# Hybrid attention layer: the two end blocks of each window share one transpose, GpSimd parts them again, and mixer B's projections stand in one planned line

## The chip, the core and the metric

The kernel runs on one core of one Trainium2 chip, in one launch. The metric is device time in microseconds (us); smaller is better. Times are medians of a few runs; the profile is one further execution, with every instruction's start and duration. Engines are PE (TensorE), DVE (VectorE), ACT (ScalarE), POOL (GpSimd) and SP (SyncE, which issues most of the transfers).

## The reference, cut to what matters

One decoder layer over 1024 tokens of width 1024. After the norm, one projection feeds two attention mixers. Mixer A (8 heads, 2 key/value groups) has three branches per query: compressed tokens (`cmp`), selected blocks (`slc`) and a sliding window of 512 keys (`win`). Mixer B (8 heads, 2 groups) has a sliding window of 128 keys (`swa`) with one learned sink per head that enters the softmax's sum alone. ALiBi distances are subtracted everywhere.

```python
def banded_attention(q, k, v, slopes, window, sinks=None):
    # 128-query blocks; keys t-window+1..t
    s = jnp.einsum('bgrnqd,bgnkd->bgrnqk', qb, kb) * (dh ** -0.5)
    valid = (dist >= 0) & (dist < window) & (kpos[:, None, :] >= 0)
    s = s - slopes[None, :, :, None, None, None] * dist.astype(jnp.float32)
    s = jnp.where(valid, s, NEG)
    if sinks is not None:
        p = jax.nn.softmax(jnp.concatenate([s, sink], axis=-1), axis=-1)[..., :-1]
    else:
        p = jax.nn.softmax(s, axis=-1)
    return jnp.einsum('bgrnqk,bgnkd->bgrnqd', p, vb)
...
o_win = banded_attention(qa, k_win, v_win, slopes_a, NSA_WINDOW)              # window 512
o_b = banded_attention(qb, kb_, vb_, slopes_b, SWA_WINDOW, sinks=sinks[l])    # window 128
```

For a 128-query block i, the window of 128 keys touches key blocks i-1 and i, and the window of 512 touches i-4 to i. In the oldest block only keys strictly above the diagonal (column j > row p) are inside the window; in block i only those with j <= p. So the two end blocks of a window together have exactly one valid key for each pair (p, j).

## The kernel before, in words

Every product of full precision is made of two parts in a rounded type: a high part and a low part (`hh`, `hl` of the input; `wh`, `wl` of the weights; `ph`, `pl` of the probabilities; V holds both halves side by side). Projections (lines L187 to L195, and L917 to L922 in `quarter`) are half blocks of 24 matmuls with 512 columns: 8 chunks of the depth, three products each.

Attention runs in four units: mixer B groups 0 and 1, then mixer A groups 0 and 1. A unit goes over its tasks (query block i, branch). A task has two steps:

- `scores`: for each of the group's four heads r, two matmuls (q with `kh` and `kl`) into a PSUM bank `s`; DVE adds the ALiBi distances and takes the row's minimum in one custom instruction (L797); ACT takes the exponential with the row's sum (L809); DVE takes the reciprocal (L813); POOL scales the row by it and by the branch's gate (L821). Distances and masks are in tables: `DC` (causal), `DW` (window of 512) and `DB` (window of 128); masked places hold 1e30.
- `weigh`: for each key block, four PE transposes (one per head, L858) into one bank `pt`; ACT copies that to `ph` (L864), DVE subtracts to get `pl` (L865); two PV matmuls of 512 columns (L866 with `ph`, L869 with `pl`) add to `pv`. After a query block's last branch, `finish` adds the two halves of `pv`, multiplies by the gate path (POOL, L880) and stores.

The `weigh` of a task is issued after the `scores` of the next. For `swa` the sink enters as the starting value of the minimum, and its term of the sum is made apart: subtract, exponential, add, then one reciprocal (L815 to L818). The rows of `slc`, and of every second `swa`, are in buffers `ps` (4 of 1024 columns), those of `win` and the other `swa` in `pw` (4 of 640 columns).

The order of each engine's queue is set when the kernel is built: attention has high priority, and projections of later stages fill PE between its steps. What limits them is `hold`: a projection may not stand before the attention matmul that lies `AHEAD` us back by a count of attention's columns (`mark`, `done`, `held`). In mixer A they stand in one line, `pieces`, cut into quarters of a half block (`Planned.quarter`), each with a due place; `pump` issues those that are due, and `owed` makes an attention step wait for a quarter that is `LAG` overdue. In mixer B, projections are issued whole after a task (`spread`, and a loop over the `late` ones).

`split_half` makes `wh` (a copy, ACT) and `wl` (a subtraction, POOL, L164) from each loaded half of weights.

## Time and profile before

| | |
|---|---|
| runs | 899.46, 900.00, 901.08 us; median 900.0 |
| profiled execution | 900.77 us, of which the span of instructions is 899.0 us |
| mean granted PE clock | 0.992 |
| mixer B's attention, first to last POOL scaling | 171.0 to 292.5 us |
| mixer A's attention | 292.5 to 694.6 us |
| POOL: weight halves `wl` (L164) | 102, 133.7 us in all |
| POOL: row scalings (L821), `ps` and `pw` and `pc` | 192 |

A row of the groups reads: line, engine, operation, output<-inputs, shapes, count, then busy us in all, mean ns of one, then idle us of the engine just before them and what ended it. A row of the timeline reads: start us, duration us, engine, line, operation, tiles, count, and in brackets the idle time before it with its releaser. Matmul durations overlap: the next one starts before the last has ended.

### The profile page before, as it was taken

To read this page: it belongs to the slowest core of one execution; us is meant where nothing else is said; L and a number is where in the kernel's file an instruction comes from. 1 tells how busy PE (TensorE), PEld (TensorE's weight loads), DVE (VectorE), ACT (ScalarE), POOL (GpSimd) and SP (SyncE) were. 2 spreads that over 40 slices of the span, in tenths; PEclk is the share of its full clock that TensorE was granted. 3 is DMA by queue.
4 is the path that set the end of the run, shared out by engine and by line. 5 is a ranking of instruction groups with operands and counts; after the bars stand their busy time and mean duration, and the time that the engine had idled before them with its cause. 6 is when DMAs were issued, how large, how long until landed. Compare 5 with 4: busy or idle time off the path is not lost.

```text
span 899.0 us, 14304 instructions
## 1 busy us (share of the span) xinstructions
PE 888.9 (99%) x4538; PEld 753.0 (84%) x4538; DVE 538.2 (60%) x1511; ACT 505.6 (56%) x1150; POOL 356.9 (40%) x428
## 2 busy tenths in 40 slices
PE   8999999999999999999999999999999999999997
PEld 7989888888888888888888888888887888887885
DVE  5866863465578677575585677566463372677322
ACT  6477732466676877565666777565464555442111
POOL 1000421365576866452544576453351366200000
PEclk7999999999999999999999999999999999999999
DMA  9873442342234332111222131211212677335432
GB/s 353 281 249 101 141 163 78 118 136 97 82 101 116 115 87 73 48 54 53 71 63 80 60 89 59 80 51 36 83 39 68 207 250 230 115 112 188 138 104 80
DMA packets 67087, 104.51 MB, mean 116 GB/s; under 512 B 8002, under 2 KB 25794, under 8 KB 67011
## 3 DMA queue, kind: packets, MB, share of 16 engines
q1 hardware_dynamic: 65856, 102.36, 35.1%
q10 hardware_dynamic: 1154, 1.23, 0.5%
q8 instruction: 36, 0.59, 0.3%
q14 instruction: 41, 0.33, 0.1%
HBM read 79.97 MB, written 19.92 MB: 111 GB/s over the span
## 4 chain that ended last, share of the span: by engine, by line
PE 95%; DVE 1%; DMA 1%; ACT 1%; issue 0%; POOL 0%; SPq 0%; DVEq 0%; POOLq 0%; ACTq 0%
PE b_pt L858 8%; PE b_pj L917 7%; PE b_pj L921 7%; PE b_pj L922 7%; PE b_pj L194 5%; PE b_pj L195 5%; PE b_pj L187 5%; PE b_s L790 5%; PE b_s L787 4%; PE b_pv L869 4%; PE b_pv L866 4%; PE b_s L1158 1%; PE b_s L1157 1%; PE b_s L1156 1%; PE b_s L1078 1%; PE b_s L1080 1%
## 5 line engine op out<-in xcount | busy, mean ns | idle before, releaser
L164 POOL TENSOR_TENSOR wl<-wraw,wh 128x512 fp32r<-128x512 f32 x102 | 133.7, 1313 | 137.7 <-ACT wh L161 86.6
L865 DVE TENSOR_TENSOR pl<-b_pt,ph 128x512 fp32r<-128x512 f32 x162 | 110.4, 687 | 63.2 <-ACT ph L864 62.3
L864 ACT CAST ph<-b_pt 128x512 fp32r<-128x512 f32 x162 | 93.8, 583 | 64.7 <-PE b_pt L858 51.2
L917 PE MATMUL b_pj<-hh,wh 128*128 128x512 f32 x288 | 117.6, 412 | 0.0
L922 PE MATMUL b_pj<-hh,wl 128*128 128x512 f32 x288 | 114.0, 396 | 0.0
L921 PE MATMUL b_pj<-hl,wh 128*128 128x512 f32 x288 | 113.1, 394 | 0.0
L821 POOL TENSOR_SCALAR ps<-ps,rr,gates 128x128 f32<-128x128 f32 (+7 forms) x64 | 52.7, 827 | 92.4 <-DVE rr L813 51.4
L194 PE MATMUL b_pj<-hl,wh 128*128 128x512 f32 x224 | 88.2, 394 | 0.0
L187 PE MATMUL b_pj<-hh,wh 128*128 128x512 f32 x224 | 88.0, 393 | 0.0
L195 PE MATMUL b_pj<-hh,wl 128*128 128x512 f32 x224 | 87.9, 393 | 0.0
L787 PE MATMUL b_s<-kh,q 128*128 128x256 f32 (+6 forms) x272 | 85.8, 323 | 0.0
L790 PE MATMUL b_s<-kl,q 128*128 128x256 f32 (+6 forms) x272 | 83.9, 316 | 0.0
L809 ACT ACTIVATE ps<-ps,mins 128x256 f32<-128x256 f32 (+7 forms) x96 | 64.9, 677 | 32.2 <-DVE mins L797 30.4
L161 ACT CAST wh<-wraw 128x512 fp32r<-128x512 f32 x94 | 57.5, 615 | 32.8 <-PE b_pj L194 11.7
L809 ACT ACTIVATE pw<-pw,mins 128x256 f32<-128x256 f32 (+4 forms) x96 | 60.7, 633 | 26.6 <-DVE mins L797 26.2
L869 PE MATMUL b_pv<-pl,V 128*128 128x512 f32 x162 | 67.5, 417 | 0.2
L866 PE MATMUL b_pv<-ph,V 128*128 128x512 f32 x162 | 65.3, 403 | 0.0
L922 PEld LDWEIGHTS b_pj<-hh,wl 128*128 128x128 f32 x288 | 54.1, 188 | 10.8
L921 PEld LDWEIGHTS b_pj<-hl,wh 128*128 128x128 f32 x288 | 54.4, 189 | 8.5
L880 POOL TENSOR_TENSOR ot<-ot,zt 64x512 f32<-64x512 f32 x32 | 41.2, 1288 | 49.9 <-DVE ot L879 41.0
L821 POOL TENSOR_SCALAR pw<-pw,rr,gates 128x640 f32<-128x640 f32 (+4 forms) x64 | 47.6, 748 | 32.4 <-DVE rr L813 18.0
L917 PEld LDWEIGHTS b_pj<-hh,wh 128*128 128x128 f32 x288 | 53.9, 189 | 7.5
(309 smaller groups left out, 2137.7 us busy)
## 6 DMA issues: line engine op xcount, KB each, us to landing
wraw<-in_w_blk SPq DMA_DIRECT2D x90, 256.0 KB, 2.9
wa<-in_w_adaT SPq DMA_DIRECT2D x23, 512.0 KB, 5.2
w1raw<-in_w SPq DMA_DIRECT2D x16, 256.0 KB, 3.4
od<-ot SPq DMA_DIRECT2D x64, 64.0 KB, 2.1
sp_MA<-sp SPq DMA_DIRECT2D x16, 256.0 KB, 2.0
wraw<-in_w_o SPq DMA_DIRECT2D x16, 256.0 KB, 3.4
wraw<-in_w_out SPq DMA_DIRECT2D x16, 256.0 KB, 3.7
t<-od SPq DMA_DIRECT2D x16, 256.0 KB, 4.0
```

The lines of the kernel that those rows point to most:

```text
L164: chain("wl", nc.gpsimd.tensor_tensor(wl, raw, wh.bitcast(F32), ALU.subtract))
L187: ins = nc.tensor.matmul(t, lhsT=wh, rhs=hh[kc][half], start=(kc == 0), stop=False)
L194: nc.tensor.matmul(t, lhsT=wh, rhs=hl[kc][half], start=False, stop=False)
L195: nc.tensor.matmul(t, lhsT=wl, rhs=hh[kc][half], start=False, stop=(kc == KC - 1))
L787: ins = nc.tensor.matmul(sp[:, :n_in], lhsT=q, rhs=rh, start=True, stop=False)
L790: nc.tensor.matmul(sp[:, :n_in], lhsT=q, rhs=rl, start=False, stop=True)
L809: nc.scalar.activation(rows[r][:, :off], rows[r][:, :off], AF.Exp, scale=-1.0, bias=last_min[:, r : r + 1], accum_out=sums[:, r : r + 1])
L865: nc.vector.tensor_tensor(pl, t, ph.bitcast(F32), ALU.subtract)
L869: nc.tensor.matmul(pv, lhsT=v, rhs=pl, start=False, stop=(last and n == len(todo) - 1))
L917: ins = nc.tensor.matmul(self.t, lhsT=wh, rhs=hh[kc][self.half], start=(kc == 0), stop=False)
L921: nc.tensor.matmul(self.t, lhsT=wh, rhs=hl[kc][self.half], start=False, stop=False)
L922: ins = nc.tensor.matmul(self.t, lhsT=wl, rhs=hh[kc][self.half], start=False, stop=(kc == KC - 1))
```

## The change

Three things are changed.

First, the two end blocks of a window become one. After the two score matmuls of a head, DVE's `copy_predicated` puts the oldest block's scores over those of block i wherever j > p (mask `first`), and the minimum, exponential, sum and scaling run over one block less. `weigh_joined` transposes the joined block (four transposes), ACT copies it to the first half of `own`, DVE writes the low part into the second half, and POOL parts the two with `affine_select`: `ahead` keeps the places of the old block, `own` those of block i, zeros elsewhere. Then four PV matmuls follow. This serves `swa` for i > 0 and `win` for i > 3. `own` and `ahead` are taken from the buffers `ps`.

Second, `swa` rows are in four tiles `four` (in `pw`'s place) with a column for the sink in each row, so that the exponential's own sum has the sink's term; the operations apart from it go, and the reciprocal is taken per head.

Third, mixer B's projections also stand in a line of quarters, with `AHEAD` 1.5 and `LAG` 2; the late ones are two each at three places of the line.

The core of the diff:

```diff
-LATE = (0.1, 0.1)
-LAG = 4
-AHEAD = 3
+AHEAD = {"B": 1.5, "A": 3}
+LAG = {"B": 2, "A": 4}
...
@@ scores
-                row = at.tile([P, width], F32, name=tag, tag=tag, bufs=4)
+                row = four[:, r, 1 : P + 1] if br == "swa" else at.tile([P, width], F32, name=tag, tag=tag, bufs=4)
...
+                    if br == "swa" and i:
+                        nc.vector.copy_predicated(sp[:, P : 2 * P], tables["first"], sp[:, :P])
+                        pre, w = P, P
+                    elif br == "win" and i > 3 and c == 0:
+                        pre, w, dist, far = P, w - P, dist[:, P:], sp
+                    elif br == "win" and i > 3:
+                        nc.vector.copy_predicated(sp[:, w - P : w], tables["first"], far[:, :P])
                     ins = nc.vector.tensor_tensor_reduce(
                         out=row[:, off : off + w], in0=sp[:, pre : pre + w], in1=dist, scale=2.0 ** -(h + 1),
                         scalar=init, op0=ALU.add, op1=ALU.min, accum_out=mins[:, c, r : r + 1])
...
-        if br == "swa":
-            nc.vector.tensor_tensor(rr, last_min, nsink[:, 4 * g : 4 * g + 4], ALU.subtract)
-            nc.scalar.activation(rr, rr, AF.Exp)
-            nc.vector.tensor_tensor(sums, sums, rr, ALU.add)
-            nc.vector.reciprocal(rr, sums)
+            if br == "swa":
+                nc.scalar.activation(
+                    four[:, r, : P + 1], four[:, r, 1 : P + 2], AF.Exp, scale=-1.0, bias=last_min[:, r : r + 1],
+                    accum_out=sums[:, r : r + 1])
+                rows[r] = four[:, r, :P]
+            else:
+                ...
+            nc.vector.reciprocal(rr[:, r : r + 1], sums[:, r : r + 1])
...
+    def weigh_joined(g, i, br, rows, off, pv):
+        vi, ends = (4 + g, (i - 1, i)) if br == "swa" else (2 + g, (i - 4, i))
+        pump()
+        t = bank("pt")
+        for r in range(4):
+            ins = nc.tensor.transpose(t[:, r * P : r * P + P], rows[r][:, off : off + P], ident)
+            if r == 0:
+                chain("pt", ins)
+                mark(ins, 3100)
+        own, ahead = (at.tile([P, S], F32R, name="pj", tag="ps", bufs=4) for _ in range(2))
+        nc.scalar.copy(own[:, :512], t)
+        nc.vector.tensor_tensor(own[:, 512:], t, own[:, :512].bitcast(F32), ALU.subtract)
+        nc.gpsimd.affine_select(
+            out=ahead, in_=own.bitcast(F32), pattern=[[0, 8], [-1, P]], compare_op=ALU.is_gt, fill=0.0,
+            base=0, channel_multiplier=1)
+        nc.gpsimd.affine_select(
+            out=own, in_=own.bitcast(F32), pattern=[[0, 8], [1, P]], compare_op=ALU.is_ge, fill=0.0,
+            base=0, channel_multiplier=-1)
+        alone = br == "swa"
+        for n, (part, b) in enumerate(zip((ahead, own), ends)):
+            v = V[b][:, vi].rearrange("p a d -> p (a d)")
+            for k in range(2):
+                ins = nc.tensor.matmul(
+                    pv, lhsT=v, rhs=part[:, 512 * k : 512 * k + 512],
+                    start=(alone and n == 0 and k == 0), stop=(alone and n == 1 and k == 1))
...
+        if br == "win" and i > 3:
+            weigh_joined(g, i, br, rows, 3 * P, pv)
...
+        if u == 0:
+            line = plan_k(g, 1, "B") + plan_q("B", 0, 1) + merges(2) + plan_q("B", 1, 0)
+        elif u == 1:
+            line = plan_q("B", 1, 1) + merges(2) + plan_k(0, 0) + plan_q("A", 0, 0) + merges(2)
...
+        if mixer == "B":
+            if g == 0:
+                fours.extend(at.tile([P, 640], F32, name="four", tag="pw", bufs=4) for _ in range(4))
+            for four in fours:
+                nc.gpsimd.tensor_copy(
+                    four.rearrange("p (r c) -> p r c", r=4)[:, :, P + 1], nsink[:, 4 * g : 4 * g + 4])
```

What moves is seen in the order of the queues. V_129 to V_136 are the values of key blocks 0 to 7, `hh_` and `hl_` the input's chunks (so those rows are projections), `b_pt` the transposes' bank, `b_pv` the output's, `pc_` the rows of the compressed branch. In the changed kernel, `weigh`'s transposes are L907 and its PV matmuls L915 and L918; the joined transposes are L865 and the joined PV matmuls L883.

PE at the end of attention, mixer A, group 1, win of i = 7, before; the blocks of keys 5, 6 and 7 come one after the other:

```order
L866 MATMUL b_pv<-ph,V_134 128x512
L869 MATMUL b_pv<-pl,V_134 128x512
L858 MATMUL b_pt<-ident,pw 128x128 x4
L866 MATMUL b_pv<-ph,V_135 128x512
L830 MATMUL b_pt<-ident,pc_1660 128x128
L830 MATMUL b_pt<-ident,pc_1654 128x128
L869 MATMUL b_pv<-pl,V_135 128x512
L866 MATMUL b_pv<-ph,V_136 128x512
L869 MATMUL b_pv<-pl,V_136 128x512
L841 MATMUL b_pv<-ph,vc_751 128x2x128 x2
L187 MATMUL b_pt<-hh_86,wh 128x512
```

The same place in the changed kernel, where the joined transposes stand and the projections of the next stage begin:

```order
L915 MATMUL b_pv<-ph,V_134 128x512
L918 MATMUL b_pv<-pl,V_134 128x512
L865 MATMUL b_pt<-ident,pw 128x128 x4
L915 MATMUL b_pv<-ph,V_135 128x512
L844 MATMUL b_pt<-ident,pc_1660 128x128
L844 MATMUL b_pt<-ident,pc_1654 128x128
L918 MATMUL b_pv<-pl,V_135 128x512
L187 MATMUL b_pt<-hh_86,wh 128x512
```

And still PE, 23 projection matmuls after those transposes:

```order
L194 MATMUL b_pt<-hl_116,wh 128x512
L883 MATMUL b_pv<-pj,V_132 128x512 x2
L195 MATMUL b_pt<-hh_100,wl 128x512
L187 MATMUL b_pj<-hh_87,wh 128x512
L194 MATMUL b_pj<-hl_103,wh 128x512
L195 MATMUL b_pj<-hh_87,wl 128x512
L883 MATMUL b_pv<-pj,V_136 128x512 x2
L855 MATMUL b_pv<-ph,vc_751 128x2x128 x2
```

The PV matmuls of key blocks 3 and 7 have moved behind the first projections of the next stage.

PE at the first joined win task, mixer A, group 0, i = 4, in the changed kernel, from the joined transposes on:

```order
L865 MATMUL b_pt<-ident,pw 128x128 x4
L968 MATMUL b_pj<-hh_99,wh 128x512
L968 MATMUL b_pj<-hh_86,wh 128x512
L972 MATMUL b_pj<-hl_102,wh 128x512
L973 MATMUL b_pj<-hh_86,wl 128x512
L968 MATMUL b_pj<-hh_88,wh 128x512
L972 MATMUL b_pj<-hl_104,wh 128x512
L973 MATMUL b_pj<-hh_88,wl 128x512
L972 MATMUL b_pj<-hl_115,wh 128x512
L973 MATMUL b_pj<-hh_99,wl 128x512
L968 MATMUL b_pj<-hh_101,wh 128x512
L972 MATMUL b_pj<-hl_117,wh 128x512
```

and directly behind it on PE, up to the first joined PV pair and the next slc scores:

```order
L973 MATMUL b_pj<-hh_101,wl 128x512
L915 MATMUL b_pv<-ph,V_132 128x512
L918 MATMUL b_pv<-pl,V_132 128x512
L844 MATMUL b_pt<-ident,pc_1656 128x128
L844 MATMUL b_pt<-ident,pc_1658 128x128
L793 MATMUL b_s<-kh,q 128x320
L796 MATMUL b_s<-kl,q 128x320
L883 MATMUL b_pv<-pj,V_129 128x512 x2
L793 MATMUL b_s<-kh,q 128x512
L796 MATMUL b_s<-kl,q 128x512
```

Before, PE's last block of that task (key block 4) stood so:

```order
L866 MATMUL b_pv<-ph,V_132 128x512
L921 MATMUL b_pj<-hl_117,wh 128x512
L922 MATMUL b_pj<-hh_101,wl 128x512
L787 MATMUL b_s<-kh,q 128x256
L790 MATMUL b_s<-kl,q 128x256
L869 MATMUL b_pv<-pl,V_132 128x512
L866 MATMUL b_pv<-ph,V_133 128x512
L787 MATMUL b_s<-kh,q 128x384
L790 MATMUL b_s<-kl,q 128x384
```

There the next scores stood before the task's last PV matmuls; now the last PV pair waits for two POOL instructions, with more projections ahead of it.

POOL in mixer B, group 0, before (with the numbers of buffers), about two tasks:

```order
L821 TENSOR_SCALAR ps_1854<-ps_1854,rr_1852 128x256
L821 TENSOR_SCALAR ps_1860<-ps_1860,rr_1852 128x256
L821 TENSOR_SCALAR ps_1866<-ps_1866,rr_1852 128x256
L821 TENSOR_SCALAR ps_1872<-ps_1872,rr_1852 128x256
L880 TENSOR_TENSOR ot_1802<-ot_1802,zt_1799 64x512
L164 TENSOR_TENSOR wl_1970<-wraw_1963,wh_1969 128x512
L164 TENSOR_TENSOR wl_2141<-wraw_2136,wh_2140 128x512
L880 TENSOR_TENSOR ot_1912<-ot_1912,zt_1909 64x512
L821 TENSOR_SCALAR pw_2005<-pw_2005,rr_2003 128x256
```

POOL in mixer B, group 0, in the changed kernel:

```order
L164 TENSOR_TENSOR wl_2015<-wraw_2008,wh_2014 128x512
L835 TENSOR_SCALAR four_1667<-four_1667,rr_1928 128x128 x2
L931 TENSOR_TENSOR ot_1921<-ot_1921,zt_1918 64x512
L835 TENSOR_SCALAR four_1667<-four_1667,rr_1928 128x128 x2
L873 AFFINE_SELECT pj_2031<-pj_2030 128x1024
L164 TENSOR_TENSOR wl_2234<-wraw_2229,wh_2233 128x512
L876 AFFINE_SELECT pj_2030<-pj_2030 128x1024
L873 AFFINE_SELECT pj_2113<-pj_2112 128x1024
L164 TENSOR_TENSOR wl_2238<-wraw_2231,wh_2237 128x512
L876 AFFINE_SELECT pj_2112<-pj_2112 128x1024
L835 TENSOR_SCALAR four_1664<-four_1664,rr_2050 128x128 x2
```

Two selects of 128x1024 per task have come between weight halves, row scalings and output products, and a scaling covers half as many columns.

111 lines of the change are left out of this document (52 added, 59 removed).

## The prediction, made before the run

> **What bounds the kernel now.** I read the page first, then the list of waits of TensorE (PE), then the busy time by stretches, then the timeline of PE in short windows, since the busy time of PE cannot be used as a price.
>
> ```profile
> PE 888.9 (99%) x4538; PEld 753.0 (84%) x4538; DVE 538.2 (60%) x1511; ACT 505.6 (56%) x1150; POOL 356.9 (40%) x428
> PE 95%; DVE 1%; DMA 1%; ACT 1%; issue 0%; POOL 0%; SPq 0%; DVEq 0%; POOLq 0%; ACTq 0%
> ```
> ```profile
> PE b_pv L333 <- POOL xr L387: 1.7, 1, 1.7
> PE b_pt L294 <- DVE eps L309: 1.0, 1, 1.0
> PE b_s L210 <- ACT hh L302: 0.6, 1, 0.6
> PE b_pt L631 <- ACT w L627: 0.2, 1, 0.2
> ```
> ```profile
> 171.00:292.50 121.50, 121.50 (x649) 103.18 (x648) 77.34 (x227) 81.71 (x219) 75.77 (x101) 1.00 0.35 105
> 292.50:694.60 402.10, 401.71 (x2191) 341.44 (x2190) 256.29 (x930) 263.50 (x648) 208.84 (x258) 1.00 0.22 68
> ```
>
> The first row is the busy time of each engine, the second the chain that ended last: 95% of it is PE. The four waits are all that PE has in the whole run, and none of their lines belongs to attention. In the two stretches (columns: length, then PE, weight loads, DVE, ACT, POOL, then granted clock, DMA share, GB/s) mixer B's attention, from its first POOL scaling to its last, has PE busy in 121.50 of 121.50 us and mixer A's in 401.71 of 402.10, at clock 1.00. DVE, ACT and POOL have a third or more to spare. So time comes off only where PE's queue gets shorter, and is lost where PE has to wait. The matmuls of projections fill every hole between a task's steps.
>
> **The price of a transpose.** The change takes transposes away, and two views price them differently.
>
> ```profile
> L858 PE MATMUL b_pt<-ident,ps 128*128 128x128 f32 x344 | 57.4, 272 | 0.0
> L858 PE MATMUL b_pt<-ident,pw 128*128 128x128 f32 x304 | 47.7, 272 | 0.0
> ```
> ```profile
> 675.96 0.60 PE L858 MATMUL b_pt<-ident,ps 128*128 128x128 f32 x4
> 676.32 0.48 PE L917 MATMUL b_pj<-hh,wh 128*128 128x512 f32 x1
> 676.63 0.39 PE L921 MATMUL b_pj<-hl,wh 128*128 128x512 f32 x1
> 676.86 0.40 PE L922 MATMUL b_pj<-hh,wl 128*128 128x512 f32 x1
> ...
> 180.10 0.39 PE L194 MATMUL b_pj<-hl,wh 128*128 128x512 f32 x1
> 180.33 0.27 PE L858 MATMUL b_pt<-ident,pw 128*128 128x128 f32 x1
> 180.35 0.48 PE L195 MATMUL b_pj<-hh,wl 128*128 128x512 f32 x1
> 180.67 0.27 PE L858 MATMUL b_pt<-ident,pw 128*128 128x128 f32 x1
> 180.70 0.48 PE L187 MATMUL b_pj<-hh,wh 128*128 128x512 f32 x1
> 181.01 0.40 PE L194 MATMUL b_pj<-hl,wh 128*128 128x512 f32 x1
> ```
>
> One lasts 272 ns, but instructions overlap: a 512-column matmul lasts 0.39 us and the next starts 0.23 later (676.63 to 676.86). What a removal frees is the distance between starts. Four transposes: 676.32 - 675.96 = 0.36, and the matmul behind them holds the queue 0.31 instead of 0.23, so 0.44 us. Singly, as in mixer B: 181.01 - 180.10 = 0.91 for three matmuls (0.69) and two transposes, so 0.11 each, the same. I take 0.44 per four. The Trainium skill, "TensorE: Matmul & The Clock Gate", Part 4 on PE-mode transpose, gives about 275 ns for one inside a kernel; as a duration the row's 272 agrees. Taken as a price it would make 88 transposes worth 24.2 us instead of 9.7, and the distances between starts speak against that.
>
> **The sum, part by part.**
>
> 1. *Joined blocks.* `weigh_joined` serves the swa tasks with i over 0 (7 x 2 = 14) and the win tasks with i over 3 (4 x 2 = 8). Each has four transposes fewer; its PV matmuls stay four (two blocks times high and low before, two blocks times two halves of 512 columns now), and so do the score matmuls. 22 x 0.44 = **-9.7 us**, 6.2 of it in B, 3.5 in A. Counting the instructions of both kernels on PE gives the same: 648 transposes of rows become 560, nothing else changes in number.
>
> 2. *The new path to PV.* It was transposes, ACT copy, PV; now it is transposes, ACT copy, DVE subtraction, one `affine_select` of 128x1024 on POOL, first PV pair, a second select, second pair. The last blocks of attention show the hand-overs:
>
> ```profile
> 691.20 0.60 PE L858 MATMUL b_pt<-ident,pw 128*128 128x128 f32 x4
> 691.83 0.59 ACT L864 CAST ph<-b_pt 128x512 fp32r<-128x512 f32 x1 [0.72 <-DVE pl L865]
> 692.45 0.69 DVE L865 TENSOR_TENSOR pl<-b_pt,ph 128x512 fp32r<-128x512 f32 x1 [0.62 <-ACT ph L864]
> ...
> 692.58 0.48 PE L866 MATMUL b_pv<-ph,V 128*128 128x512 f32 x1
> ...
> 693.20 0.44 PE L830 MATMUL b_pt<-ident,pc 128*128 128x128 f32 x2
> ```
>
> From the first transpose's start to the end of the subtraction: 692.45 + 0.69 - 691.20 = 1.94 us, gaps of about 0.03 included. 0.44 of this PE spends on the transposes themselves, so it needs other work for 1.5 + 0.06 + x, where x is the select. For x the trace has one short relative:
>
> ```profile
> masks.py:199 POOL TENSOR_SCALAR_AFFINE_SELECT ident<-ident 128x128 f32<-128x128 f32 x1 | 0.3, 294 | 0.1
> masks.py:197 POOL MEMSET ident<- 128x128 f32 x1 | 0.2, 206 | 0.3 <-POOLq L1265 0.3
> L1265 POOL MEMSET const-float32-1.0<- 128x1 f32 x1 | 0.1, 99 | 0.0
> L821 POOL TENSOR_SCALAR ps<-ps,rr 128x128 f32<-128x128 f32 x8 | 2.8, 376 | 7.0 <-DVE rr L818 7.0
> L821 POOL TENSOR_SCALAR pw<-pw,rr 128x256 f32<-128x256 f32 x32 | 14.8, 482 | 8.8 <-DVE rr L818 5.9 <-PE b_s L790 1.9 <-PE b_pt L858 1.0
> L164 POOL TENSOR_TENSOR wl<-wraw,wh 128x512 fp32r<-128x512 f32 x102 | 133.7, 1313 | 137.7 <-ACT wh L161 86.6 <-DVE wh L158 43.6 <-PE b_s L1080 2.8
> ```
>
> The scaling grows by 482 - 376 = 106 ns per 128 columns, the memset by 206 - 99 = 107 ns. At that slope the select of 1024 columns takes 294 + 7 x 106 = 1.04 us: the low end. If only the 99 ns of a one-column memset are fixed in the 294, the slope is 195 ns per 128 and x = 1.66; if nothing is fixed, 8 x 294 = 2.35: the high end (the two-input wl subtraction grows no faster). I take **1.05**, since two one-input operations share that slope, and keep 1.66 and 2.35 for the rivals.
>
> In A's first joined task (order above) 12 projection matmuls, 2 PV, 2 short transposes and 2 scores lie between the joined transposes and the first pair: about 3.7 us against 1.56 + 1.05 = 2.6. By the same count the eight A tasks leave 3.7 to 5.9 us for the first pair; the tightest second pair (win 7 of group 0, with one scaling of about 0.45 between the selects) has 4.4 against 4.2. B's 14 leave 6 us and more. Cover exists, thin at one or two places: **+0.5 us** (0 to 3).
>
> 3. *POOL in B.* It is in-order, and loses 56 x (482 - 376) = 5.9 us on halved rows, gains 28 selects and eight 4-column copies (about 1 us): 75.8 - 5.9 + 1.0 + 28x = 70.9 + 28x. At 1.05 that is 100 us in a stretch of 121.5 - 6.2 = 115.3, 87% instead of 62%. Weight halves (wl), row scalings and `ot` wait behind the selects; they have several us of lead. **+0.4 us** (0 at best). POOL fills the stretch at x = 44.4 / 28 = 1.59. In A it stays near 55%.
>
> 4. *DVE and ACT.*
>
> ```profile
> L865 DVE TENSOR_TENSOR pl<-b_pt,ph 128x512 fp32r<-128x512 f32 x162 | 110.4, 687 | 63.2 <-ACT ph L864 62.3
> L797 DVE CUSTOM_DVE_ANT_0 pw<-b_s,tab,nsink 128x256 f32<-128x256 f32 x32 | 14.7, 476 | 11.2 <-PE b_s L790 10.9 <-PE b_pt L858 0.3
> L797 DVE CUSTOM_DVE_ANT_0 ps<-b_s,DC,nsink 128x128 f32<-128x128 f32 x8 | 2.6, 346 | 8.6 <-PE b_s L790 5.5 <-DMA DC<-in_DC 3.0
> L652 DVE COPY kcf<-b_pt 128x126 f32<-128x126 f32 x1 | 0.3, 289 | 1.2 <-PE b_pt L649 1.2
> L864 ACT CAST ph<-b_pt 128x512 fp32r<-128x512 f32 x162 | 93.8, 583 | 64.7 <-PE b_pt L858 51.2
> ```
>
> 88 `copy_predicated` of 128x128 enter DVE, at about a PSUM copy's 289 ns (bounds 0.2 and 0.35): +25 us. Out go 22 subtractions x 687 (15 us) and 88 reductions shorter by 128 columns, about 0.13 each (11 us). The sink's three small operations per task go and three reciprocals come, a few us less. DVE is even, ACT loses 22 x 583 and shorter exponentials, some 25 us. Neither bounds PE: **0**. Covered by PE's projections; without those each row's exponential would start about 0.2 us later.
>
> 5. *One line of projections in B.* The same half blocks are now cut into quarters between attention's steps; PE's count is unchanged, no DMA is added, and SP's queue has 468 instructions in both. B's PE had no hole to close: **0** (a few tenths either way).
>
> 6. *End of attention.* Before, the last blocks run without filler: 691.20 + 0.36 to 693.20 holds two PV starts that waited for copies. The joined block is moved behind 23 projection matmuls and leaves three such blocks: **-0.4 us** (0 to -1.2).
>
> Sum: -9.7 + 0.5 + 0.4 - 0.4 = **-9.2 us**. The profiled execution took 900.77 us (span 899.0 and 1.8 around it), which is 0.8 above the median of 900.0; it becomes 891.6, and against the median I forecast **890.8 us**. A difference within 0.2% (1.8 us) is no change that this measurement can tell.
>
> **The rivals.**
>
> *POOL fills up in B.* At x = 1.66, POOL needs 70.9 + 28 x 1.66 = 117.4 us where PE needs 115.3: +2.1, and in A the tight second pairs come about 1 us late, twice: 900 - 10.1 + 4.1 = 894; with in-order waits on top, up to 898. For it: the select writes another type and follows a two-level pattern, which the short one did not. Against: the common slope. The Trainium skill, "GPSIMD Engine Reference", section 3.1, lets a loop with three or more operations per element run at about 1.8 cycles, 769 ns for 512 elements; by that the select would take about 1.54 us as an estimate, and POOL 114 of B's 115.3 us.
>
> *Slower: POOL becomes the bound.* At x = 2.35 it needs 136.7 us in B, +21.4; in A first pairs miss by 0.2 and the tight second ones by 2 to 3, some +6: 900 - 10.1 + 27 = 917. It decides from 28 (x - 1.59) = 10.1 + 1.8, x about 2.0. Against: it asks that nothing in the 294 ns be fixed, while a one-column memset takes 99.
>
> *No change: the ring of `ps`.* `own` and `ahead` take two of the four `ps` buffers, so in A the next slc task's rows 2 and 3 cannot be reduced by DVE before the second PV pair; reductions of later rows queue behind them. If each of the seven tasks with a successor lost about 1.2 us so, the gain would be gone: 900. Against: projection matmuls stand in PE's order there.
>
> *More: the duration is the price.* 24 us, 876; against it the starts above.
>
> **How the numbers follow.** Forecast case 0.67 (own range 888 to 894), POOL filled 0.13 (894 to 898), slower 0.09 (902 to 918), no change 0.07, more 0.04. The first two hold 0.8: range 888 to 898. Faster 0.67 + 0.13 + 0.04 = 0.84, same 0.07, slower 0.09.
>
> **What would show it.** Right: starts of projection matmuls still 0.23 apart, PE without waits at the joined PV line, 560 transposes at 272 ns, selects near 1.05 us, POOL below 90% in B, B's stretch about 6 us and A's about 3.5 us shorter. Wrong: selects above 1.6 us, or PE waiting for POOL at the PV line, or DVE waiting for PE before reductions into `ps`.

## The result and the profile after

The changed kernel is slower: 910.66 us median (907.91 to 911.24, four runs) against 900.54 for the kernel before on the same chip, a ratio of 1.0108 with a 95% interval of 1.0089 to 1.0127. The profiled execution took 911.03 us, with a span of 909.3 (before: 900.77 and 899.0). The forecast was 890.8, with a range of 888 to 898.

From the page of the changed kernel, the busy times and the chain that ended last. PE is busy about as long as before, with 88 instructions fewer, and its share of the chain fell from 95% to 85%; DVE, DMA, ACT and plain issue took the rest:

```profile
PE 890.0 (98%) x4450; PEld 746.4 (82%) x4450; DVE 533.0 (59%) x1597; ACT 481.2 (53%) x1108; POOL 393.8 (43%) x480
PE 85%; DVE 5%; DMA 4%; ACT 2%; issue 2%; POOL 1%; DVEq 0%; ACTq 0%; SPq 0%; POOLq 0%
```

The rows of attention in the list of PE's waits, changed kernel (total us, times, longest). Before, no wait of attention stood in it; now four do, and L187 of the next phase waits for attention's last block:

```profile
PE b_pj L968 <- DVE kl L525: 4.3, 1, 4.3
PE b_s L793 <- DVE mins L811: 3.3, 5, 2.1
PE b_s L793 <- DVE minc L817: 1.1, 2, 0.6
PE b_pt L187 <- DVE pj L871: 0.7, 1, 0.7
PE b_s L793 <- DVE b_s L810: 0.4, 2, 0.2
```

Busy time by stretches of the changed kernel (length, PE, weight loads, DVE, ACT, POOL, granted clock, DMA share, GB/s). Two stretches of 20 us stand out: PE is busy 15.73 and 17.24 of 20.00, and the mean clock fell to 0.91 and 0.83. POOL has 15 of 100 us free from 200 us on, most of it B:

```profile
180.00:200.00 20.00, 15.73 (x73) 12.96 (x72) 10.86 (x37) 10.50 (x27) 12.25 (x16) 0.91 0.40 115
200.00:300.00 100.00, 100.00 (x511) 83.63 (x511) 63.08 (x234) 58.59 (x161) 84.54 (x110) 1.00 0.35 105
300.00:470.00 170.00, 168.62 (x895) 141.30 (x895) 107.26 (x409) 106.59 (x276) 95.07 (x120) 1.00 0.22 71
470.00:490.00 20.00, 17.24 (x76) 14.02 (x76) 15.57 (x59) 12.10 (x29) 10.91 (x13) 0.83 0.17 53
```

The first and the last of these stretches in the kernel before:

```profile
180.00:200.00 20.00, 20.00 (x108) 16.82 (x107) 12.92 (x34) 13.82 (x36) 13.25 (x16) 1.00 0.49 142
470.00:490.00 20.00, 20.00 (x116) 17.11 (x116) 12.29 (x45) 13.03 (x32) 10.66 (x14) 1.00 0.26 80
```

The groups that answer to the transposes and the select of the forecast (instructions, busy us, mean ns, idle before). Most transposes last 272 or 273 ns, as before; with L865's 32 of A and 8 more at L907 there are 560 of them; the selects take 1.09 us:

```profile
L907 PE MATMUL b_pt<-ident,ps 128*128 128x128 f32 x288 | 47.2, 273 | 0.0
L907 PE MATMUL b_pt<-ident,pw 128*128 128x128 f32 x176 | 27.2, 272 | 0.1
L865 PE MATMUL b_pt<-ident,four 128*128 128x128 f32 x56 | 13.5, 287 | 0.0
L873 POOL TENSOR_SCALAR_AFFINE_SELECT pj<-pj 128x1024 fp32r<-128x1024 f32 x22 | 24.0, 1090 | 53.5 <-DVE pj L871 48.4 <-PE b_pj L973 3.8 <-DVE rr L832 1.2
L876 POOL TENSOR_SCALAR_AFFINE_SELECT pj<-pj 128x1024 fp32r<-128x1024 f32 x22 | 24.0, 1092 | 0.5
```

To put a size on each place I use one measure for all kernels, worked out from the starts of PE's matmuls in each trace: every matmul is given the distance to the next start that its shape has where nothing waits (226.5 ns for 512 columns, 117 for 256, 109 for a transpose, and so on), and what the real distance has above that is *lost*. The sum of the usual distances is PE's work. From 868.5 us it fell to 859.1, by 9.4: the gain of the forecast is there. The measure itself prices each transpose at 109 ns, so what shows that the price holds is a stretch without waits: from 180 to 280 us e5 below, which has the joined blocks, lies only 1.4 us above the usual distances (1.1 before). The lost time rose from 22.6 to 42.5, by 19.9. Together +10.5, and the span grew by 10.3. Below are all kernels; each ratio is to runs of the kernel before on the same chip, while the lost times are those of the one profiled execution, which can lie elsewhere in the scatter than the median. "A's late tiles" are the stretches 400 to 520 and 600 to 720 us, in which six of the eight joined windows are scored, and the last column holds the beginning, 520 to 600 us and the end of the kernel. The beginning alone moves by about 1 us either way between kernels that do not differ there.

| kernel | median us | ratio to before, 95% interval | PE's work | lost 180-280 | 280-400 | A's late tiles | rest |
|---|---|---|---|---|---|---|---|
| before | 900.5 | 1 | 868.5 | 1.1 | 1.6 | 4.5 | 15.4 |
| changed | 910.66 | 1.0108 [1.0089, 1.0127] | 859.1 | 7.4 | 3.2 | 16.5 | 15.4 |
| e1 copy on ACT | 903.55 | 1.0036 [1.0023, 1.0048] | 859.1 | 4.7 | 1.9 | 12.3 | 15.9 |
| e2 B's projections as before | 909.73 | 1.0104 [1.0088, 1.0120] | 859.1 | 1.5 | 7.4 | 17.6 | 14.6 |
| e3 e1 and e2 | 906.52 | 1.0065 [1.0048, 1.0083] | 858.7 | 1.5 | 7.5 | 13.3 | 15.8 |
| e4 before, planned line | 907.18 | 1.0074 [1.0061, 1.0087] | 868.8 | 4.9 | 1.9 | 5.0 | 18.1 |
| e5 e1, key block first | 898.58 | 0.9980 [0.9971, 0.9988] | 859.2 | 1.4 | 1.7 | 12.1 | 15.5 |
| e6 e1, joined in B alone | 902.77 | 1.0029 [1.0018, 1.0040] | 862.5 | 7.4 | 3.1 | 5.6 | 15.7 |
| e7 joined in A alone | 906.03 | 1.0067 [1.0052, 1.0082] | 865.2 | 1.1 | 1.8 | 13.4 | 14.5 |
| e8 e5, joined in B alone | 897.46 | 0.9968 [0.9956, 0.9981] | 862.6 | 1.4 | 2.1 | 5.5 | 15.4 |
| e9 e8, bank held | 899.03 | 0.9978 [0.9969, 0.9987] | 862.3 | 1.4 | 2.1 | 6.7 | 16.2 |
| e10 e8, copy without hold | 897.84 | 0.9965 [0.9951, 0.9978] | 862.7 | 1.4 | 2.0 | 5.7 | 15.7 |
| e11 e5, far block to SBUF | 903.29 | 1.0030 [1.0018, 1.0043] | 858.9 | 1.4 | 1.7 | 16.9 | 16.3 |
| e12 before, copy on ACT | 899.75 | 0.9994 [0.9985, 1.0004] | 868.6 | 1.1 | 1.6 | 4.6 | 14.3 |
| e13 e5, four weight buffers | 903.7 | 1.0020 [1.0007, 1.0032] | 859.1 | 1.6 | 1.7 | 12.1 | 21.3 |
| e14 e13, own ring | 904.61 | 1.0047 [1.0032, 1.0062] | 858.8 | 1.4 | 9.3 | 7.1 | 15.8 |
| e15 e5, no window select | 900.50 | 1.0000 [0.9991, 1.0010] | 858.8 | 1.4 | 1.8 | 13.2 | 17.0 |
| e16 e13, own ring for windows | 896.71 | 0.9956 [0.9941, 0.9970] | 858.8 | 1.5 | 1.8 | 7.4 | 19.7 |

Two large stalls carry most of the loss, and they do not have the same cause. The first is at B's start. The timeline of the changed kernel there (start, duration, engine, line, operands, and in brackets the idle time before it and its releaser):

```profile
186.53 1.14 ACT L161 CAST wh<-wraw 128x512 fp32r<-128x512 f32 x2 [2.12 <-PE b_pj L972]
187.50 0.40 PE L973 MATMUL b_pj<-hh,wl 128*128 128x512 f32 x1
187.58 0.57 ACT L517 CAST kh<-b_pj 64x512 fp32r<-64x512 f32 x1
190.05 0.58 ACT L517 CAST kh<-b_pj 64x512 fp32r<-64x512 f32 x1
191.24 1.26 POOL L931 TENSOR_TENSOR ot<-ot,zt 64x512 f32<-64x512 f32 x1
191.29 1.25 DVE L523 CAST kh<-kc 128x64 fp32r<-128x64 f32 x1
192.57 0.69 DVE L525 TENSOR_TENSOR kl<-b_pj,kh 64x512 fp32r<-64x512 f32 x1
193.32 0.58 PE L968 MATMUL b_pj<-hh,wh 128*128 128x512 f32 x1 [4.27 <-DVE kl L525]
```

The first product of the next query block (L968) needs a `pj` bank, and there are two. One still holds the key block: its first copy to SBUF (L517) starts at 187.58, since on ACT it stands behind two casts of later weights that waited 2.12 us for PE. The order in which PE has the products tells why the bank is full so late. It is quoted from the changed kernel (1705 is the key block's bank, 1839 the query block's):

```
859 L968 MATMUL b_pj_1839<-hh6_99,wh_1701 128x512
860 L972 MATMUL b_pj_1839<-hl6_115,wh_1701 128x512
861 L973 MATMUL b_pj_1705<-hh6_99,wl_1690 128x512
862 L973 MATMUL b_pj_1839<-hh6_99,wl_1702 128x512
863 L968 MATMUL b_pj_1705<-hh7_101,wh_1689 128x512
864 L968 MATMUL b_pj_1839<-hh7_101,wh_1701 128x512
865 L972 MATMUL b_pj_1705<-hl7_117,wh_1689 128x512
866 L972 MATMUL b_pj_1839<-hl7_117,wh_1701 128x512
867 L973 MATMUL b_pj_1705<-hh7_101,wl_1690 128x512
```

The key block's last four products, from the one of chunk 6 with the low weights `wl_1690` on, were put behind nearly all of the query block's 24. Both banks fill at the same time and are emptied at the same time.

The second is in A. The same columns, changed kernel:

```profile
475.21 1.29 POOL L931 TENSOR_TENSOR ot<-ot,zt 64x512 f32<-64x512 f32 x1
476.34 2.62 DVE L523 CAST kh<-kc 128x64 fp32r<-128x64 f32 x1 [0.56 <-PE b_s L793]
476.48 1.19 POOL L835 TENSOR_SCALAR ps<-ps,rr,gates 128x1024 f32<-128x1024 f32 x1
477.64 1.26 POOL L164 TENSOR_TENSOR wl<-wraw,wh 128x512 fp32r<-128x512 f32 x1
478.87 0.68 DVE L811 CUSTOM_DVE_ANT_0 ps<-b_s,DC 128x512 f32<-128x512 f32 x1
479.61 0.44 PE L793 MATMUL b_s<-kh,q 128*128 128x384 f32 x1 [2.12 <-DVE mins L811]
```

A copy of 128x64 on DVE, SBUF to SBUF, lasts 2.62 us. It starts while POOL is at work and ends with the end of three POOL instructions that follow each other without a gap (476.50, 477.67, 478.90). DVE's minimum (L811), which frees a score bank, comes after it, and PE waits. The slow clock that follows doubles the price: for 6.8 us from 480.3 on the granted clock is 0.50, so about 3.4 us of what is lost here are lost to the clock. At B's start it is 0.50 for 3.4 us from 193.6 on, about 1.7 us.

### The profile page after: what moved, and what is told of

Same layout as the page of the kernel before. It is cut to its first block, busy times and chain, and to the rows that moved or that the text cites. A ratio compares the mean times of both kernels' runs of the same rounds, so it can differ in the third digit from the quotient of the medians.

```text
span 909.3 us, 14092 instructions
## 1 busy us (share of the span) xinstructions
PE 890.0 (98%) x4450; PEld 746.4 (82%) x4450; DVE 533.0 (59%) x1597; ACT 481.2 (53%) x1108; POOL 393.8 (43%) x480
## 4 chain that ended last, share of the span: by engine, by line
PE 85%; DVE 5%; DMA 4%; ACT 2%; issue 2%; POOL 1%; DVEq 0%; ACTq 0%; SPq 0%; POOLq 0%
PE b_pj L968 10%; PE b_pj L972 10%; PE b_pj L973 10%; PE b_pt L907 5%; PE b_s L793 5%; PE b_s L796 4%; PE b_pv L918 3%; PE b_pv L915 3%; PE b_pj L194 2%; PE b_pv L883 2%; PE b_pj L195 2%; PE b_pj L187 2%; DMA t<-sp_MA 2%; PE b_s L1202 1%; PE b_s L1201 1%
## 5 line engine op out<-in xcount | busy, mean ns | idle before, releaser
L968 PE MATMUL b_pj<-hh,wh 128*128 128x512 f32 x408 | 165.8, 409 | 4.3 <-DVE kl L525 4.3
L973 PE MATMUL b_pj<-hh,wl 128*128 128x512 f32 x408 | 162.2, 398 | 0.0
L972 PE MATMUL b_pj<-hl,wh 128*128 128x512 f32 x408 | 161.9, 397 | 0.0
L914 DVE TENSOR_TENSOR pl<-b_pt,ph 128x512 fp32r<-128x512 f32 x118 | 80.5, 688 | 73.3 <-ACT ph L913 73.0
L973 PEld LDWEIGHTS b_pj<-hh,wl 128*128 128x128 f32 x408 | 77.3, 189 | 16.2
L968 PEld LDWEIGHTS b_pj<-hh,wh 128*128 128x128 f32 x408 | 77.0, 190 | 16.3 <-DVE kl L525 4.5
L793 PEld LDWEIGHTS b_s<-kh,q 128*128 128x128 f32 x272 | 51.8, 190 | 16.4 <-DVE mins L811 5.4
L829 ACT ACTIVATE ps<-ps,mins 128x128 f32<-128x128 f32 (+7 forms) x64 | 49.6, 776 | 21.3 <-DVE mins L811 18.3
L832 DVE RECIPROCAL rr<-sums 128x1 f32<-128x1 f32 x256 | 38.3, 158 | 35.1 <-ACT pw L829 14.6
L835 POOL TENSOR_SCALAR pw<-pw,rr,gates 128x512 f32<-128x512 f32 (+3 forms) x64 | 43.7, 689 | 32.1 <-DVE rr L832 31.1
L796 PEld LDWEIGHTS b_s<-kl,q 128*128 128x128 f32 x272 | 52.0, 192 | 5.3
L829 ACT ACTIVATE pw<-pw,mins 128x512 f32<-128x512 f32 (+3 forms) x64 | 41.0, 642 | 18.2 <-DVE mins L811 18.2
L918 PE MATMUL b_pv<-pl,V 128*128 128x512 f32 x118 | 49.2, 417 | 0.1
```

Source lines behind the costliest of these rows:

```text
L793: ins = nc.tensor.matmul(sp[:, :n_in], lhsT=q, rhs=rh, start=True, stop=False)
L796: nc.tensor.matmul(sp[:, :n_in], lhsT=q, rhs=rl, start=False, stop=True)
L829: nc.scalar.activation(rows[r][:, :off], rows[r][:, :off], AF.Exp, scale=-1.0, bias=last_min[:, r : r + 1], accum_out=sums[:, r : r + 1])
L835: nc.gpsimd.tensor_scalar(rows[r][:, :off], rows[r][:, :off], rr[:, r : r + 1], gate, ALU.mult, ALU.mult)
L914: nc.vector.tensor_tensor(pl, t, ph.bitcast(F32), ALU.subtract)
L918: nc.tensor.matmul(pv, lhsT=v, rhs=pl, start=False, stop=(last and n == len(todo) - 1))
```

## The experiments

### Where the large stalls come from

Theory: the copy at L523 is held back while POOL works (A's stall, 6.3 us with the slow clock behind it), and the line's order makes B's. Rival: the ring of `ps` makes A's.

**e1**, one line:

```
-nc.vector.tensor_copy(khp[:, pre - 64 : pre], kc2[:, 0, keys[r][1], :].bitcast(F32))
+nc.scalar.copy(khp[:, pre - 64 : pre], kc2[:, 0, keys[r][1], :].bitcast(F32))
```

> The changed kernel with one edit: the four copies of 128x64 at L523 are made by ScalarE instead of VectorE. In the changed kernel's trace they take 1.25, 2.47, 2.13 and 2.62 us on VectorE (0.18 to 1.22 before), while GpSimd is working without a gap beside them, and TensorE's largest stall in band A (2.28 us at 477.2, with 6.3 us lost against the nominal distances from 460 to 500 us) begins during the longest. Theory (VectorE's copy is held back while GpSimd works, and TensorE's stalls at 477 and 341 come from that): the loss of 460 to 500 us goes (-6.3), most of that of 340 to 360 (-1.4) and about 1 us of the 4.4 at 188.8: 901 to 904 us. Rival (the four-buffer ring ps that own and ahead now share makes band A's stalls): no change by more than 1.5 us, 909 to 912. Rival (the lower clock in those stretches is a limit of its own on a denser TensorE): the loss comes at another place, 909 to 912.

Measured 903.55 us, 7.1 below the changed kernel. The line L523 in the kernel before, the changed kernel and e1 (shortest, middle and longest duration of four, in ns):

```profile
L523 DVE CAST kh<-kc x4: 179/192/1217, 189.9 to 461.4; 128x64 fp32r<-128x64 f32 x4
```
```profile
L523 DVE CAST kh<-kc x4: 1254/2303/2617, 191.3 to 476.3; 128x64 fp32r<-128x64 f32 x4
```
```profile
L523 ACT CAST kh<-kc x4: 231/238/244, 193.5 to 474.6; 128x64 fp32r<-128x64 f32 x4
```

The theory holds for this part. A's late tiles lose 12.3 instead of 16.5 (4.2 less, where 6.3 were expected from 460 to 500 us), 280 to 400 loses 1.9 instead of 3.2, and B's start 2.7 less. The copies of the low halves (L524) stayed on DVE. One of them lasts 3.03 us in e1, at 271.4, and PE is busy in every one of the 20 us from 260 to 280: a copy held back costs time only where PE soon needs what DVE does next. The control is **e12**, the same edit in the kernel before:

> The kernel before with L523's four copies on ScalarE, a control for e1: three of them took 0.2 us and one 1.2 us there, and TensorE did not wait for them. If e1's 7 us were the joined blocks' doing: within 1 us of the kernel before, 899.5 to 901.5. If ScalarE suits these copies better whatever stands beside them: 896 to 898.

899.75 us, a ratio of 0.9994 that holds 1. Before the change the copy cost nothing that can be measured.

**e2** puts B's projections back (whole blocks at steps, no planned line in B), **e3** both:

```
-line = plan_k(g, 1, "B") + plan_q("B", 0, 1) + merges(2) + plan_q("B", 1, 0)
...
+spread(own + q_fills(mixer, g, 1), 0, 3 * nt // 8)
...
+spread(nk + q_fills(m2, g2, 0), nt // 2, nt)
```

> The changed kernel with band B's projections placed as in the kernel before (whole, at steps, no planned line in B); the joined blocks stay in both bands. Theory (the stall of 4.4 us at 188.8 and the slow clock behind it, 6.1 us lost from 180 to 200, come from the line: the key block's bank is emptied only after two casts of weights for later blocks): 904 to 906 us, and no wait of more than 0.5 us on a pj bank in B; A's losses stay. Rival (the stall comes from the joined blocks, whose copies and selects fill ScalarE and GpSimd at B's start, as the forecast's term of 0 for the line has it): 909 to 912, with a like stall near 190.

> Both edits: L523's copies on ScalarE, and B's projections placed as in the kernel before. If the two losses are separate and both causes hold: 13 to 14 us below the changed kernel, 896 to 899 us, so some 2 to 4 us faster than the kernel before. If only one of them holds: 903 to 906. If neither: 909 to 912. The forecast's 891 would need the remaining 4 to 5 us of band A (stretches near 411, 441, 611 and 645) to go too.

909.73 and 906.52 us, 4 and 8 above the upper ends of what was expected. e2's time lies where the rival had put it, but without the rival's stall near 190: the stall at B's start is gone (1.5 lost from 180 to 280), and 7.4 are lost from 280 to 400 instead. In e3's timeline ACT waits for the one `ot` buffer to be stored, and the last joined copy of B (L871) waits behind it:

```profile
294.23 0.58 ACT L930 COPY ot<-b_pv 64x512 f32<-64x512 f32 x1 [2.45 <-DMA od<-ot]
294.84 0.68 DVE L931 TENSOR_TENSOR ot<-b_pv,ot 64x512 f32<-64x512 f32 x1 [2.34 <-ACT ot L930]
295.57 0.59 ACT L871 CAST pj<-b_pt 128x512 fp32r<-128x512 f32 x1 [0.24 <-PE b_pt L866]
297.89 1.09 POOL L874 TENSOR_SCALAR_AFFINE_SELECT pj<-pj 128x1024 fp32r<-128x1024 f32 x1
299.38 1.09 POOL L877 TENSOR_SCALAR_AFFINE_SELECT pj<-pj 128x1024 fp32r<-128x1024 f32 x1
```

Its two selects then stand on POOL ahead of the first scalings of A. e7 below, with the same projections but B weighed block by block, loses only 1.8 there. So beside the joined blocks neither placing is free: the old projections stall at the passage from B to A, the line at B's start.

**e4**, the planned line alone in the kernel before:

> The kernel before with the planned line of projections in B alone: no joined blocks, the sink as before. Theory (the line's order is what stalls, with or without the joined blocks): +4 to +6 us against the kernel before, 904 to 907 us, with a wait on a pj bank near 190. Rival (the line stalls only beside the joined blocks): within 1.5 us of the kernel before, 899 to 902. The forecast's term for the line was 0, the same as this rival.

907.18 us. The line costs 6.4 us without any joined block, in 180 to 280 (4.9 lost) and, in smaller waits, from 520 on. The wait on a `pj` bank that was expected near 190 is not there. Casts of later weights stand in ACT's queue and wait for PE as in the changed kernel, and here a query's second half is late (timeline of e4):

```profile
196.76 1.14 ACT L160 CAST wh<-wraw 128x512 fp32r<-128x512 f32 x2 [1.60 <-PE b_pj L920]
197.93 0.60 ACT L501 ACTIVATE q<-b_pj 64x512 fp32r<-64x512 f32 x1
201.00 1.41 DVE L502 SCALAR_TENSOR_TENSOR q<-b_pj,q 64x512 fp32r<-64x512 f32 x2
201.74 0.39 PE L786 MATMUL b_s<-kh,q 128*128 128x256 f32 x1 [1.22 <-DVE q L502]
```

In e4 too one copy of 128x64 on DVE (there L522) is held back beside POOL, 2.43 us at 186.97. Whether it has a part in the 4.9 us is not shown: no run has the line alone with the copies on ACT.

**e5** is e1, with a planned block's first product in B tied behind the last product of the block in front:

```
 ins = nc.tensor.matmul(self.t, lhsT=wh, rhs=hh[kc][self.half], start=(kc == 0), stop=False)
...
+if k == 0 and behind is not None:
+    after(ins, behind)
```

> The kernel of e1 (L523's copies on ScalarE, else as changed) with one more edit: in band B a planned block's first product may not come ahead of the last product of the block in front of it. In the changed kernel's order the last five products of the key block's bank stand between and behind the query block's own, so both pj banks are full until 187.5 us, and their copies to SBUF follow two casts of later weights on ScalarE. Theory (this order makes the stall of 3.3 us that e1 still has at 190.5): the loss of 180 to 200 us falls from 3.6 to under 1, 900 to 901.5 us. Rival (the copies are late because ScalarE and VectorE are full at B's start, whatever the order): the wait moves to another product of the same stretch, 902.5 to 904.5.

898.58 us, 5.0 below e1 and below the kernel before. The first L517 now starts at 182.97 instead of 187.58, and the stretch of B's start has no idle time on PE:

```profile
180.00:200.00 20.00, 20.00 (x103) 16.65 (x102) 13.44 (x47) 13.44 (x35) 16.96 (x22) 1.00 0.41 119
```

The order made the stall: 3.3 us of the 5.0 by the table (4.7 to 1.4); the rest lies in small differences elsewhere and in the scatter.

### What the joined windows of A lose

After e5, A's late tiles still lose 12.1 us where the kernel before loses 4.5. **e6** (e1) and **e8** (e5) join in B alone; **e7** joins in A alone, with B and its projections as before:

```
-        if br == "win" and i > 3:
-            weigh_joined(g, i, br, rows, 3 * P, pv)
```

> The kernel of e1 with the joined blocks in band B alone: the windows of band A are weighed block by block as before, so 8 of 22 joined pairs go. TensorE gets 8 x 0.44 = 3.5 us of products and transposes back. Theory (the losses that e1 still has in A, 15.2 us from 320 to 720 us against 7.0 in the kernel before, come from the joined windows, whose first score bank is held until the second one's predicated copy): 903.55 + 3.5 - 8.2 = 898 to 900 us. Rival (these losses come from how the plan of A's line counts its columns, which stays): 906 to 908.

> The edits of e5 and e6 together: joined blocks in B alone, L523's copies on ScalarE, the key block's products ahead of the query block's. If the three losses (VectorE's copy, the order of the two blocks, the joined windows) are separate: 895 to 897 us, below the kernel before by 4 to 6. If the order isn't what stalls B's start: 898 to 900. If the joined windows aren't what loses in A: 902 to 905.

> The joined blocks in band A alone: band B weighed, its sink and its projections as before, L523's copies on ScalarE. If the windows lose more (8.2 us of waits) than they save (3.5 us): 904 to 907 us. Rival (without the joined blocks of B beside it, the join of the windows pays what its transposes are worth): 896.5 to 898.5. The forecast's own size for this part, 8 pairs at 0.44 us: 897.3.

e7 came out at 906.03, as the first theory said: the windows' 3.3 us of saved work cost 8.9 in waits. In e6 and e8 the late tiles lose 5.6 and 5.5, so beside the joined blocks of B the joined windows are worth about 6.6 us of waits. e6 itself missed its number (902.77 for 898 to 900): its stall at B's start was e1's (3.1 us by the list of waits in both), but the clock behind it was not, and it also lost 1.2 us more from 280 to 400, which stays open. e1, then e6:

```profile
180.00:200.00 20.00, 16.91 (x86) 13.99 (x86) 10.81 (x38) 10.80 (x30) 14.79 (x19) 1.00 0.43 121
```
```profile
180.00:200.00 20.00, 16.91 (x73) 13.89 (x72) 9.90 (x36) 10.41 (x28) 12.59 (x17) 0.83 0.42 115
```

e8 was just above its expectation of 895 to 897, and below the kernel before.

**e9** and **e10** take e8 and add to each row of the windows of tiles 4 to 7 a predicated copy that changes nothing; in e9 it reads the row's first score bank, and so holds it, in e10 its own:

```
+nc.vector.copy_predicated(sp[:, w - P : w], zeros.bitcast(mybir.dt.int32), far[:, :P])   # e9
+nc.vector.copy_predicated(sp[:, w - P : w], zeros.bitcast(mybir.dt.int32), sp[:, :P])    # e10
```

> The kernel of e8 (windows weighed block by block, 897.5 us) with one instruction more per row of a window of tiles 4 to 7: a predicated copy of 128x128 whose mask is all zero, from the first score bank of the row into the second, so that nothing changes but VectorE's 0.29 us and that the first bank is held until the second bank's products are done, as in the joined windows. Theory (the joined windows lose 6.5 us, 12.1 against 5.6 from 400 to 520 and 600 to 720 us, because one of three score banks is held longer): +4 to +7 us against e8, 901 to 905, with TensorE's L793 line waiting for VectorE at the same places. Rival (the loss comes from VectorE's added time alone): the same as in e10. Rival (it comes from the selects, the scalings or the ring of ps that the joined blocks share): within 1 us of e8.

> As e9, but the copy with the all-zero mask reads the second bank itself, so no bank is held longer and only VectorE's 32 x 0.29 = 9.3 us are added. Theory (the held bank): within 1 us of e8, 896.5 to 898.5. Rival (VectorE's added time): like e9, 901 to 905.

899.03 and 897.84; e9 stays below the theory's 901 to 905. The held bank costs about 1.2 us in the late tiles (6.7 against 5.5 in e8) and DVE's added time 0.2. My theory of the bank fell as the main cause; it explains a fifth.

**e11** frees the bank in the full version (e5) by a copy of the far block to SBUF:

```
+nc.vector.tensor_copy(far, sp[:, :P])        # far = row[:, 4 * P : 5 * P]
 nc.vector.copy_predicated(sp[:, w - P : w], tables["first"], far)
```

> The kernel of e5 (joined blocks in both bands, 898.6 us) with the far block's 128 columns copied to SBUF on VectorE (32 copies of 128x128, the free end of the pw row) as soon as the first bank's products are done; the predicated copy then reads SBUF, and the first bank is free after its own minimum. Theory (the held bank): most of the 6.5 us in A's later tiles goes, less what the copies cost VectorE (32 x 0.2 to 0.3): 892 to 896 us. Rival (VectorE's time is what is short there): 899 to 903. A predicated copy whose mask and source both lie in SBUF may also be held back by GpSimd, as the copies of L523 were: then it takes more than 0.29 us in the trace, and the gain is lost.

903.29 us, 4.7 above e5. What the expectation feared came true: with mask and source in SBUF one predicated copy lasted 1.96 us, while POOL worked without a gap from 436.98 to 440.57, and PE waited 1.9 us right behind it. Most of the 32 copies kept their 0.3 us, so DVE's added time (the rival) may have a part in the loss as well. The predicated copies of the windows in the changed kernel, with the source in PSUM, and in e11 (shortest, middle, longest):

```profile
L810 DVE COPY_PREDICATED b_s<-tab,b_s x32: 274/294/297, 371.9 to 684.9; 128x128 f32<-128x128 int32 x32
```
```profile
L811 DVE COPY_PREDICATED b_s<-tab,pw x32: 278/296/1960, 366.7 to 679.8; 128x128 f32<-128x128 int32 x32
```

**e13, e14 and e16** test the ring of `ps`. Two more buffers of 4 KB do not fit beside six buffers for weights, so all three have four, which frees 8 KB (the expectation of e13 says 16, which is wrong). e13 is the control; in e14 `own` and `ahead` have two buffers of their own, in e16 only those of the windows:

```
-own, ahead = (at.tile([P, S], F32R, name="pj", tag="ps", bufs=4) for _ in range(2))
+tag, bufs = ("oa", 2) if br == "win" else ("ps", 4)      # e16; e14: always ("oa", 2)
+own, ahead = (at.tile([P, S], F32R, name="pj", tag=tag, bufs=bufs) for _ in range(2))
```

> Control for e14: the kernel of e5 (898.6 us) with four instead of six buffers each for the high and low weights, which frees 16 KB of SBUF. own and ahead still take two of the four ps buffers. Fewer weights ahead can only cost: 898 to 905 us, and TensorE's stalls in A's later tiles (400 to 520 and 600 to 720 us, 12.1 us lost in e5, 5.6 in e8 without joined windows) stay.

> As e13, with own and ahead in two buffers of their own, 8 KB, so that the next tile's slc rows find all four ps buffers. In e5 those rows' minima follow the second joined product of the window before (402.8 us, then DVE at 403.8), and TensorE's stalls come 11 to 13 us behind each window's select. Theory (the shared ring makes the loss of 6.5 us in the joined windows, the forecast's rival of no change): 4 to 6 us below e13, and 5 to 7 us lost in those stretches. Rival (GpSimd's selects and their latency put the joined products late whatever buffers they use): within 1.5 us of e13, 11 to 13 us lost. Rival (the held score bank, 1.2 us by e9): the same as the second.

> As e13 (four weight buffers), with own and ahead of band A's windows alone in two buffers of their own; band B's stay in ps, so the order up to A's start should stay as in e13, without the stall of 4.6 us at 313.8 that e14 met there (ScalarE's copy into the single ot buffer waiting for the store of the one before). Theory (the shared ring makes 5 of the 6.5 us lost in A's joined windows): 5 to 7 us lost from 400 to 520 and 600 to 720 us where e13 loses 12.1, and 4 to 6 us below e13: 897 to 900. Rival (e14's smaller loss in those stretches came only from another order behind its stall): 11 to 13 us lost there, within 1.5 us of e13.

e14: the late tiles lose 7.1 instead of 12.1, but the median is no better (904.61 against 903.7; the profiled executions, from which the lost times come, took 902.1 and 905.2). A's start lost 7.6 more, again at the single `ot` buffer (e14's timeline):

```profile
317.23 0.58 ACT L929 COPY ot<-b_pv 64x512 f32<-64x512 f32 x1 [4.63 <-DMA od<-ot]
318.58 0.80 PE L915 MATMUL b_pv<-ph,V 128*128 128x512 f32 x1 [4.40 <-DVE ot L930]
```

e16 keeps B's order, and there the gain shows: 7.4 lost in the late tiles, and 896.71 us against 903.7. e13's runs scatter from 899.5 to 905.2, so the ratios to before are the safer measure: 0.9956 against 1.0020, 0.64% or 5.8 us. How the ring works is seen at the first joined window. PE and POOL in e13, then in e16:

```profile
392.45 1.09 POOL L873 TENSOR_SCALAR_AFFINE_SELECT pj<-pj 128x1024 fp32r<-128x1024 f32 x1 [3.82 <-DVE pj L871]
394.49 0.62 PE L883 MATMUL b_pv<-pj,V 128*128 128x512 f32 x2
394.95 0.40 PE L793 MATMUL b_s<-kh,q 128*128 128x512 f32 x1
398.44 0.63 PE L883 MATMUL b_pv<-pj,V 128*128 128x512 f32 x2
398.90 0.39 PE L793 MATMUL b_s<-kh,q 128*128 128x512 f32 x1
```
```profile
389.59 0.48 PE L793 MATMUL b_s<-kh,q 128*128 128x512 f32 x1
390.14 0.31 PE L793 MATMUL b_s<-kh,q 128*128 128x320 f32 x1
393.32 1.09 POOL L874 TENSOR_SCALAR_AFFINE_SELECT pj<-pj 128x1024 fp32r<-128x1024 f32 x1 [2.69 <-DVE pj L872]
```

In e13 the next tile's slc rows 2 and 3 (the products of 512 columns) stand right behind the first and the second joined pair, each freeing one of the four buffers. In e16 all slc products are through before 391, ahead of the select. In e13 what the window of the next tile needs is then pressed together, and PE, DVE and the three score banks wait for each other (stalls from 403.7 us on).

**e15** leaves the selects of the windows out:

> The kernel of e5 without the two selects of each joined window in A, whose products then take the unselected tile twice: this leaves the parting of the two blocks out, and ahead's buffer with it; own still takes one of the four ps buffers. If GpSimd's selects (8 x 2.2 us) and the chain behind them are what loses: 4 to 6 us below e5, 892 to 895. If it is the ring alone: some of it, 895 to 898, since one buffer of two is given back. If neither: 898 to 899.5.

900.50 us, 13.2 lost in the late tiles, no better than e5. POOL's selects are not the cause, and giving back one buffer of two does not help.

e16 is the fastest version here, 0.44% below the kernel before, though its profiled execution (899.24 us) loses 7.0 us from 720 us on, where e5 loses 1.6. The medians of e13 and e5 put the price of four weight buffers at 0.40% or 3.6 us; a version with the windows' own ring and six weight buffers would by that take about 893 us, an estimate. It does not fit into SBUF, and no run has it.

## Why the prediction was wrong, point by point

The forecast was 9.2 us less, the result 10.1 us more. The saving came as forecast; what failed are terms that stood at or near nothing: DVE's 0 (step 4, with POOL in step 3), where copies held back beside POOL cost 7.1 us by e1; the line's 0 (step 5), 3.3 us here by its order; and the path's +0.5 (step 2), where the shared ring cost about 5.

- *Step 1, joined blocks, -9.7.* Right. PE's work fell by 9.4 us, by the distances between starts and not by the durations of the transposes.
- *Step 2, the path to PV, +0.5.* The hand-over itself was right: the selects take 1.09 us (1.05 estimated), and the products at L883 stand nowhere in the changed kernel's list of waits. What the step did not count are the buffers that this path holds. The ring of `ps` stood among the rivals with the right mechanism, 0.07 and a price of 8.4; it cost 5.0 (12.1 to 7.1, e14) or 4.7 (12.1 to 7.4, e16). My objection, that projection products stand in PE's order there, was true and beside the point: the order itself is made with the ring, so the slc rows were put late. The held score bank, 1.2 us, stood nowhere.
- *Step 3, POOL in B, +0.4.* The share was about right (84.5 of the 100 us from 200 on; 87% of B forecast), the consequence wrong. I asked only whether POOL fills up. A few POOL instructions without a gap between them hold a copy of DVE back long before POOL is full: 7.1 us by e1. Of the 8.2 us of lost time that went with it, 2.7 lay at B's start and 5.5 in A, where POOL was busy little more than half of the time (95.07 of 170 us from 300 to 470).
- *Step 4, DVE and ACT, 0.* The predicated copies take 0.29 us, as estimated. DVE has time to spare, yet its order is fixed, and one copy that lasts 2.62 us stops PE through the minima behind it (the same copy took 1.22 before, the other three 0.18 to 0.20).
- *Step 5, one line of projections, 0.* This is the step that failed by itself. The reason given, that PE had no hole to close and nothing changes in number, says nothing on what the order does to two `pj` banks and to ACT's queue. The line costs 6.4 us alone (e4), by other waits than in the changed kernel. In the changed kernel 3.3 us of the 6.3 at B's start are the order of two blocks (e5), nearly all of the rest the copy at L523 with the slow clock (2.7 by e1). The other half of the truth is e3 against e5: once ordered rightly, the line is worth 7.9 us to the joined blocks, which stall at A's start without it.
- *Step 6, end of attention, -0.4.* It is about +0.4: 680 to 720 us lost 1.6 before and 2.0 after, since the next phase now waits 0.7 us for the last joined subtraction (L187 for L871).

The account of the 19.9 us lost: 8.2 by the copy (2.7, 1.3 and 4.2 in the table's stretches), 3.3 by the order, 4.7 to 5.0 by the ring, 1.2 by the held bank. The parts were measured in different kernels, so that they add up is no proof. The 2 to 3 us left are not assigned; by the table most of them lie in A's late tiles, and none in the last column, which did not change.

Of the signs named as wrong, none stood out: the selects stayed below 1.6 us, PE did not wait for POOL at the joined products, and DVE's waits for PE before reductions into `ps` came to 10.4 us (18.8 before, when half of `swa` was in `ps` too). The ring cost its 5 us all the same. PE's waits stand at other lines than I looked for: where a buffer comes free, not where the new work is.

## What to carry to other kernels

When a change gives an engine work without a gap, look at every instruction of the other engines that it can hold back, and not only at its total. When a new path borrows buffers of an old ring, count who else needs them before the path's last reader, and read from the order whether their products were put behind it. That a change of order adds no instruction does not make it free: find the banks and the in-order queue that each block passes.
